# A gated-DeltaNet and RWKV-7 layer on one core: half of the triangular solver's transfers issued by ScalarE instead of SyncE

## The chip, the cores and the metric

The kernel runs on one core of one Trainium2 chip. The metric is the device time of one execution in microseconds (us). TensorE (PE) multiplies matrices, VectorE (DVE), ScalarE (ACT) and GpSimd (POOL) do the elementwise work, and SyncE (SP) has no arithmetic: here it issues transfers. Each engine takes its own instructions strictly in the order in which the program lists them, and waits for another engine, or for a transfer, on semaphores. An instruction that waits holds all that stand behind it on its engine. A transfer is carried out by the core's 16 DMA engines; the engine that issues it is free again once it has issued it.

## The reference

One layer over 512 latent tokens and 256 context tokens of width 2048. A modulated RMSNorm is followed by one input projection. Its columns feed eight gated-DeltaNet heads of width 128 and sixteen RWKV-7 heads of width 64. Both mixers run over the tokens in both directions, context first. Then come a gated output projection, the residual sum and a last RMSNorm. What matters here is the triangular system inside each chunk of 64 tokens:

```python
lmat = jnp.where(strict, jnp.einsum('bhncd,bhnsd->bhncs', kb, k) * decay, 0.0)
eye = jnp.eye(CHUNK, dtype=jnp.float32)
tmat = lax.linalg.triangular_solve(eye + lmat, jnp.broadcast_to(eye, lmat.shape),
                                   left_side=True, lower=True, unit_diagonal=True)
u = tmat @ (v * beta[..., None])
wk = tmat @ (kb * jnp.exp(g)[..., None])
...
def step(state, inp):
    u_i, wk_i, attn_i, q_i, k_i, gl_i = inp
    v_new = u_i - wk_i @ state
    o_i = q_i @ state + attn_i @ v_new
    state = state * jnp.exp(gl_i)[..., None, None] + jnp.einsum('bhcd,bhce->bhde', k_i, v_new)
    return state, o_i
```

The kernel brings RWKV-7 into the same chunked form, so that both mixers need the inverse of unit lower triangular 64x64 blocks, for both directions.

## The kernel before, in words

The heads are worked on in eight slots: a slot has one DeltaNet head and two RWKV-7 heads. Each slot is run twice, first over the context (phase 0, four chunks) and then over the latents (phase 1, eight chunks). So there are sixteen mixers: context slots 0 to 7 and then latent slots 0 to 7. The stages of a mixer are listed in `mixer`: the preparation of both branches (`prep_g`, `prep_r`, `prep_d 0`, `blocks 0`, `prep_d 1`, `blocks 1`), then `send`, `late_g`, `late_r`, `solve`, `levels`, `chain`, and for latents `outp`.

The solver is made of four of them. `blocks` leaves the triangular blocks of direction d in the tile `Z`. `send` gathers the 32x32 diagonal blocks of `Z` into the DRAM tile `DA` with eight transfers, one for each block row b (0 to 3) and direction d (0, 1). `solve` reads `DA` back into `solNL`, with one small matrix on each partition, inverts all of them on DVE in thirty steps of two instructions (`solT` and `solNL`), and writes the inverses and their transposes to the DRAM tile `DD` in one transfer. `levels` reads `DD` back with twelve transfers: for each b one into the tile `RT` (its name in the rows is `lt`) and two into `Z`. Two groups of small matmuls then make the off-diagonal blocks, and ACT and DVE write these into `Z`. `chain` runs over the chunks in order, with a state that goes from one step to the next (`Xs`, `SV`, `vt`, `vn`, `SG` and `Sbd` are its tiles).

Beside the mixers lies work that doesn't depend on them. In phase 0 it is the projections of both streams, in the beginning of phase 1 the rest of the projections, and after that the passes of the output projection. All of it splits each float32 weight tile into a high part `wh` (ACT) and a low part `wl` (DVE or POOL) and runs three matmuls for each product (`accl` and `accc` are the accumulators in the rows).

The order of the instructions is not the order of the code. Every operation is recorded (`record`) with a duration and with its dependences, and `schedule` places all of them by a model of the engines; `emit` writes them in that order. Where PE would have little to do, `schedule` puts in matmuls on a tile of zeros (`wm<-zero` in the rows). They compute nothing that is used. All transfers are recorded on SP with 475 ns each. Since one helper issues every operation, all rows of the profile have one line, L705, and the names tell them apart.

Of the kernel before, what the change touches and what calls it, by code (L numbers as in the profile page):

```python
# [148 lines left out]
OWN = {"V": 120, "A": 148, "G": 107, "S": 1500}  # L149
# [117 lines left out]

class Op:
    __slots__ = ("eng", "fn", "args", "kw", "npred", "succ", "ready", "dur", "tiles", "need", "prio", "idx", "src",
                 "end", "ps", "bytes", "key", "hold", "rows", "passes", "sync", "pos", "load", "fill", "bun", "cells", "cls", "lock")  # L270

    def clone(self):
        o = Op()
# [7 lines left out]
class Rec:  # L281
# [22 lines left out]
    def new(self, eng, fn, args, kw):  # L304
        o = Op()
        o.eng, o.fn, o.args, o.kw = eng, fn, args, kw
        o.npred, o.succ, o.ready, o.tiles, o.need, o.end, o.bytes = 0, [], 0.0, [], [], None, 0
        o.sync, o.load, o.pos, o.fill = [], 0, -1, self.fill if eng == "T" else 0
        o.idx = len(self.ops)
        o.key = o.idx + self.shift  # L310
        o.bun = self.bun if eng == "T" else None
        if o.bun:
            o.bun.ops.append(o)
        o.src = Rec.hook() if Rec.hook else None
        self.ops.append(o)
        return o
# [35 lines left out]
    def record(self, eng, fn, args, kw):  # L352
        o = self.new(eng, fn, args, kw)
        outs, ins = [], []
# [9 lines left out]
        for views, wr in ((ins, False), (outs, True)):  # L364
            for v in views:
                t = v.t
# [11 lines left out]
                for rec in t.acc:  # L378
                    a, apm, afm, aw = rec
# [12 lines left out]
        o.lock = 0  # L392
        o.sync = [a for a, sync in preds.items() if sync and a.eng != eng]
        for a, sync in preds.items():
            if a.eng == eng:
                lat = OWN.get(eng, -1) if sync else -1
            else:
                lat = LAT.get(a.eng + eng, 0) if sync else 0
            self.edge(a, o, lat)
        g = (outs[0] if outs else args[0]).shape if True else None  # L400
        n = int(np.prod(g[1:])) if len(g) > 1 else 1
# [22 lines left out]
        elif eng == "V":  # L424
            x2 = fn.startswith("tensor_scalar") or fn == "tensor_copy"
            x2 = x2 and all(v.t.pool.space != PSUM for v in outs + ins)
            two = sum(v.t.pool.space != PSUM and int(np.prod(v.shape[1:])) > 1 for v in ins) > 1
            o.lock = 2 if x2 else 1 if two else 0
            if fn == "tensor_tensor_scan":
                n *= 2  # L430
            if fn == "reciprocal":
                n *= 7
            if fn == "tensor_reduce":
                n = int(np.prod(ins[0].shape[1:]))
            o.dur = 65 + n / (1.92 if x2 else 0.96) + (62 if sc else 0)
        elif eng == "A":
            sv = isinstance(kw.get("scale"), View) and isinstance(kw.get("bias"), View)
            sc = "accum_out" in kw or any(isinstance(kw.get(a), View) for a in ("scale", "bias"))
            o.dur = (51 if args[1].t.pool.space == PSUM else 93) + 93 * sc + 0.834 * n
        elif eng == "G":  # L440
            o.lock = 1 if fn == "memset" else 2
            a, b = {"memset": (35, 0.84), "tensor_copy": (120, 3.34), "tensor_scalar": (130, 3.8)}.get(fn, (148, 2.104))
            if fn == "tensor_tensor" and any(v.g.ap[-1][0] == 0 for v in ins):
                b = 1.667
            o.dur = (298 + 165 * n) if ALU.pow in args else a + b * n
        elif eng == "S":
            o.dur = 475
            o.bytes = 4 * int(np.prod(args[0].shape)) * (2 if min(run(v) for v in outs + ins) < 128 else 1)

    def schedule(self):  # L450
        ops = self.ops
        end = {}
# [85 lines left out]
        while True:  # L538
# [109 lines left out]
            if e == "P":  # L648
                p = o.args[0]
                if o.fn == "open":  # L650
                    for k, t in p.tags.items():
# [1 line left out]
                        for x in t[1]:  # L653
                            x.free = s
                        wake(p, k)
            if e == "S":
                st = max(fin + 650, dfree)
                dfree = st + o.bytes / 360.0
                fin = dfree + 900
# [9 lines left out]
            extra += o is not ops[o.idx]  # L669
            for t in o.tiles:  # L670
                t.left -= 1
                t.last = max(t.last, fin + (200 if e != "S" else 0))
                if t.left == 0:
                    t.slot.free = t.last
                    wake(t.pool, t.key)
# [35 lines left out]
def run(v):  # L711
    n = 1
    for s, m in list(v.g.ap)[::-1][:len(v.g.ap) - (v.t.pool.space != DRAM)]:
        if m > 1 and s != n:
            break
        n *= m
    return n
# [6 lines left out]
class Mix:  # L724
# [251 lines left out]
    def send(self):  # L976
        k, i, ph, nj, S = self.k, self.i, self.ph, self.nj, self.k.S
        DA, DD = self.DD = [k.dp.tile([w, 4, 2, 3 * nj, 32, 32], F32, tag=f"{t}{ph}", bufs=2, name=k.nm(t))
                            for t, w in (("DA", 1), ("DD", 2))]
        DA = DA[0]  # L980
        for b in range(4):
            for d in range(2):
                S.dma_start(DA[b, d].rearrange("u s t -> s u t"), self.zdiag(b, d))

    def solve(self):
        k, i, ph, nb = self.k, self.i, self.ph, self.nb
# [18 lines left out]
    def levels(self):  # L1005
# [3 lines left out]
        RT = self.t2("lt")[:, 0:96 * nj].rearrange("p (u t) -> p u t", t=32)  # L1009
        for b in range(4):  # L1010
            bb = b % 2
            S.dma_start(RT[32 * b:32 * b + 32], (DN, DL)[bb][b, bb].rearrange("u s t -> s u t"))
            for d in range(2):
                S.dma_start(self.zdiag(b, d), (DL, DN)[d][b, d].rearrange("u s t -> s u t"))
        FC = (slice(32, 64), slice(0, 32))
        px = k.pmt("lx", "g")[:, 0:96 * nj].rearrange("p (u t) -> p u t", t=32)
        with k.rec.bundle():
# [927 lines left out]
```

## Time and profile before

| what | us |
|---|---|
| three runs, median (lowest to highest) | 2066.45 (2064.42 to 2070.24) |
| the profiled execution, its own time | 2065.16 |
| its span | 2063.4 |
| PE busy in it | 1932.1 |
| DVE busy | 1451.6 |
| ACT busy | 811.6 |
| POOL busy | 575.9 |

The span is what the profile covers of the execution; 1.8 us lie around it. Busy times of one engine add up to at most the span. The filler matmuls on zeros count as PE busy. DMA-issuing instructions are not counted as busy on the engine that issues them; rows that begin with SPq have them with their start and the time that they took to issue. The time to landing of a transfer is counted from its issue.

### The profile page before, as it was taken

To read this page: it belongs to the slowest core of one execution; us is meant where nothing else is said; L and a number is where in the kernel's file an instruction comes from. 1 tells how busy PE (TensorE), PEld (TensorE's weight loads), DVE (VectorE), ACT (ScalarE), POOL (GpSimd) and SP (SyncE) were. 2 spreads that over 40 slices of the span, in tenths; PEclk is the share of its full clock that TensorE was granted. 3 is DMA by queue.
4 is the path that set the end of the run, shared out by engine and by line. 5 is a ranking of instruction groups with operands and counts; after the bars stand their busy time and mean duration, and the time that the engine had idled before them with its cause. 6 is when DMAs were issued, how large, how long until landed. Compare 5 with 4: busy or idle time off the path is not lost.

```text
span 2063.4 us, 43525 instructions
## 1 busy us (share of the span) xinstructions
PE 1932.1 (94%) x16575; PEld 1501.0 (73%) x16576; DVE 1451.6 (70%) x3397; ACT 811.6 (39%) x2127; POOL 575.9 (28%) x751
## 2 busy tenths in 40 slices
PE   7999999999999999999999999979778898889997
PEld 5678887877878787777777777767656666666666
DVE  5437587787877678684775784676678877778557
ACT  4443324333232433333443343444435362534335
POOL 0004314223150512100211211245234443343235
PEclk8999999999999999999999999999899999999998
DMA  8964343434333432344543454456232545143732
GB/s 313 362 215 132 107 118 97 111 85 109 91 102 94 106 111 66 99 112 133 159 137 86 120 144 112 125 171 205 74 82 56 164 143 153 52 110 105 257 107 93
DMA packets 230514, 269.28 MB, mean 131 GB/s; under 512 B 117280, under 2 KB 130080, under 8 KB 226208
## 3 DMA queue, kind: packets, MB, share of 16 engines
q1 hardware_dynamic: 230304, 266.49, 43.9%
q8 instruction: 130, 2.13, 0.4%
q14 instruction: 80, 0.66, 0.1%
HBM read 210.50 MB, written 55.89 MB: 129 GB/s over the span
## 4 chain that ended last, share of the span: by engine, by line
PE 68%; DVE 17%; DMA 6%; issue 3%; ACT 3%; POOL 2%; SPq 1%; DVEq 0%; ACTq 0%; POOLq 0%
PE accl L705 37%; PE accc L705 9%; PE br L705 8%; PE wm L705 7%; PE pss L705 7%; DVE solNL L705 3%; DVE Gk L705 2%; DVE solT L705 2%; DVE t L705 1%; SPq L705 1%; POOL gw L705 1%; DVE Z L705 1%; DMA solNL<-DA 1%; DMA gw<-wada 1%; DVE wl L705 1%
## 5 line engine op out<-in xcount | busy, mean ns | idle before, releaser
L705 ACT ACTIVATE wh<-wr 128x512 fp32r<-128x512 f32 x312 | 196.3, 629 | 398.5 <-PE accl L705 180.6
L705 PE MATMUL accl<-hhi,wl 128*128 128x512 f32 x768 | 314.2, 409 | 4.7 <-DVE wl L705 4.7
L705 PE MATMUL accl<-hhi,wh 128*128 128x512 f32 x768 | 310.9, 405 | 1.8 <-issue 1.8
L705 PE MATMUL accl<-hlo,wh 128*128 128x512 f32 x768 | 307.9, 401 | 0.0
L705 DVE TENSOR_TENSOR wl<-wr,wh 128x512 fp32r<-128x512 f32 x264 | 189.6, 720 | 105.7 <-ACT wh L705 99.5
L705 PE MATMUL accl<-yh,wh 128*128 128x512 f32 x480 | 207.8, 435 | 11.0 <-DVE Rr L705 5.4
L705 PE MATMUL accl<-yh,wl 128*128 128x512 f32 x480 | 199.6, 416 | 0.0
L705 PE MATMUL accl<-yl,wh 128*128 128x512 f32 x480 | 197.2, 411 | 0.4 <-POOL yl L705 0.4
L705 DVE TENSOR_TENSOR solNL<-solNL,solT 48x30 f32<-48x30 f32 (+29 forms) x480 | 171.4, 357 | 10.6
L705 PEld LDWEIGHTS accl<-hhi,wl 128*128 128x128 f32 x768 | 144.5, 188 | 41.7 <-DVE wl L705 6.6
L705 POOL TENSOR_TENSOR SRd<-Sbd,Dd 64x128 f32<-64x128 f32 x160 | 67.2, 420 | 379.1 <-DVE Sbd L705 372.9
L705 DVE TENSOR_TENSOR solT<-solNL 48x30 f32<-48x30 f32 (+29 forms) x480 | 165.8, 346 | 10.0
L705 PEld LDWEIGHTS accl<-hhi,wh 128*128 128x128 f32 x768 | 144.4, 188 | 20.9 <-issue 4.8
L705 PEld LDWEIGHTS accl<-hlo,wh 128*128 128x128 f32 x768 | 144.6, 188 | 19.7 <-issue 3.3
L705 PE MATMUL accc<-clo,wh 128*128 128x256 f32 x512 | 147.8, 289 | 0.0
L705 PE MATMUL accc<-chi,wh 128*128 128x256 f32 x512 | 146.2, 286 | 0.0
L705 PE MATMUL accc<-chi,wl 128*128 128x256 f32 x512 | 146.1, 285 | 0.0
L705 PE MATMUL wm<-zero 128*128 128x128 bf16 x1326 | 105.8, 232 | 22.8 <-DVE SG L705 7.7
L705 PEld LDWEIGHTS <-zero 128*128 128x128 bf16 x1344 | 91.2, 105 | 40.7 <-issue 36.1
L705 PEld LDWEIGHTS accl<-yh,wh 128*128 128x128 f32 x480 | 91.2, 191 | 36.6 <-issue 11.3
L705 PEld LDWEIGHTS accc<-clo,wh 128*128 128x128 f32 x512 | 96.4, 188 | 23.3 <-issue 0.5
L705 PEld LDWEIGHTS accc<-chi,wh 128*128 128x128 f32 x512 | 96.5, 189 | 20.8 <-issue 0.3
(320 smaller groups left out, 4139.2 us busy)
## 6 DMA issues: line engine op xcount, KB each, us to landing
wr<-win SPq DMA_DIRECT2D x256, 256.0 KB, 3.2
wa<-wada SPq DMA_DIRECT2D x32, 1024.0 KB, 6.3
gw<-wada SPq DMA_DIRECT2D x64, 256.0 KB, 3.5
ud<-Gk SPq DMA_DIRECT2D x64, 256.0 KB, 2.9
wr<-wout SPq DMA_DIRECT2D x64, 256.0 KB, 3.6
Rk<-ud SPq DMA_DIRECT2D x48, 256.0 KB, 3.0
rtd<-xt SPq DMA_DIRECT2D x48, 256.0 KB, 3.1
Rr<-rtd SPq DMA_DIRECT2D x48, 256.0 KB, 3.1
```

The lines of the kernel that those rows point to most:

```text
L705: r = getattr(self.engs[o.eng], o.fn)(*args, **kw)
```

## The change

The four transfers of `send` for direction 1, and the six transfers of `levels` for the block rows 1 and 3, are issued by ACT. All others stay on SP. Each mixer thus has 10 transfers on ACT, and all sixteen have 160. The model of `schedule` learns that an operation of any engine can be a transfer (the new field `dq`): on ACT it takes 300 ns of the engine, on SP 475 ns as before, and its landing is modelled in the same way. Everything else is recorded as before, but since `schedule` places all operations anew, the order of the instructions changes on every engine.

```diff
@@ def new
+        o.dq = fn == "dma_start"
@@ def record
-            if a.eng == eng:
-                lat = OWN.get(eng, -1) if sync else -1
+            src, dst = "S" if a.dq else a.eng, "S" if o.dq else eng
+            if src == dst == "S" or (a.eng == eng and not a.dq):
+                lat = OWN.get(src, -1) if sync else -1
             else:
-                lat = LAT.get(a.eng + eng, 0) if sync else 0
+                lat = LAT.get(src + dst, 0) if sync else 0
...
+        elif o.dq:
+            o.dur = 475 if eng == "S" else 300
+            o.bytes = 4 * int(np.prod(args[0].shape)) * (2 if min(run(v) for v in outs + ins) < 128 else 1)
...
-        elif eng == "S":
-            o.dur = 475
-            o.bytes = 4 * int(np.prod(args[0].shape)) * (2 if min(run(v) for v in outs + ins) < 128 else 1)
@@ def schedule
-            if e == "S":
+            if o.dq:
                 st = max(fin + 650, dfree)
                 dfree = st + o.bytes / 360.0
                 fin = dfree + 900
...
-                t.last = max(t.last, fin + (200 if e != "S" else 0))
+                t.last = max(t.last, fin + (0 if o.dq else 200))
@@ def send
         for b in range(4):
             for d in range(2):
-                S.dma_start(DA[b, d].rearrange("u s t -> s u t"), self.zdiag(b, d))
+                (S, k.A)[d].dma_start(DA[b, d].rearrange("u s t -> s u t"), self.zdiag(b, d))
@@ def levels
         for b in range(4):
             bb = b % 2
-            S.dma_start(RT[32 * b:32 * b + 32], (DN, DL)[bb][b, bb].rearrange("u s t -> s u t"))
+            q = (S, k.A)[b % 2]
+            q.dma_start(RT[32 * b:32 * b + 32], (DN, DL)[bb][b, bb].rearrange("u s t -> s u t"))
             for d in range(2):
-                S.dma_start(self.zdiag(b, d), (DL, DN)[d][b, d].rearrange("u s t -> s u t"))
+                q.dma_start(self.zdiag(b, d), (DL, DN)[d][b, d].rearrange("u s t -> s u t"))
```

What stands on the engines can be shown at latent slot 4. On SP, this is the read-back of `levels` before (`lt` and `Z` out of `DD`; `lr`, `Rk` and `rtd` belong to other work):

```order
L705 DMA lr_0_9325<-lorad_114 96x512
L705 DMA lt_0_9336<-DD_0_124 32x12x32
L705 DMA Z_0_9361<-DD_0_124 32x12x32 x2
L705 DMA lt_0_9336<-DD_0_124 32x12x32
L705 DMA Z_0_9361<-DD_0_124 32x12x32 x2
L705 DMA lt_0_9336<-DD_0_124 32x12x32
L705 DMA Z_0_9361<-DD_0_124 32x12x32 x2
L705 DMA lt_0_9336<-DD_0_124 32x12x32
L705 DMA Z_0_9361<-DD_0_124 32x12x32 x2
L705 DMA Rk_0_9311<-ud_115 128x512
```

and the same place on SP now:

```order
L707 DMA lr_0_9310<-lorad_114 96x512
L707 DMA lt_0_9321<-DD_0_124 32x12x32
L707 DMA Z_0_9346<-DD_0_124 32x12x32 x2
L707 DMA lt_0_9321<-DD_0_124 32x12x32
L707 DMA Z_0_9346<-DD_0_124 32x12x32 x2
L707 DMA Rr_1_12537<-rtd_117 128x512
```

Twelve transfers have become six, and the transfer behind them follows at once. The other six now stand on ACT, between the split of a weight tile (`wh`) and a tanh of the preparation of slot 5 (`t`):

```order
L707 ACTIVATE wh_1_1437<-wr_1_1434 128x512
L707 DMA lt_0_9321<-DD_0_124 32x12x32
L707 DMA Z_0_9346<-DD_0_124 32x12x32 x2
L707 DMA lt_0_9321<-DD_0_124 32x12x32
L707 DMA Z_0_9346<-DD_0_124 32x12x32 x2
L707 ACTIVATE t_2_9306<-br_1_135,dv_66 128x512
L707 ACTIVATE xt_1_12539<-accl_0_144 128x512
```

The second place is where `chain` of slot 4 begins, on ACT. `Z<-pss` is the last step of `levels`, `Xs`, `vt`, `SV` and `vn` are the chain's first step, and `VO`, `junk` and `t` prepare slot 5. Before:

```order
L705 ACTIVATE xt_1_12492<-accl_0_144 128x512
L705 ACTIVATE Z_0_9361<-pss_0_130 32x12x32 x2
L705 ACTIVATE VO_0_12497<-br_1_135 64x4x128 x2
L705 ACTIVATE junk_0_9317,rk_0_9326<-br_0_134 128x128 x4
L705 ACTIVATE t_3_9322<-Rk_0_9311,par_62 128x512
L705 ACTIVATE Xs_0_9342<-pss_0_130 128x256
L705 ACTIVATE vt_0_9345<-wm_0_129,BT_0_71 128x128
L705 ACTIVATE vn_0_9346<-wm_0_129,BS_0_70 128x128
L705 ACTIVATE SV_0_9369<-pss_0_130 64x128
```

and now:

```order
L707 ACTIVATE xt_1_12539<-accl_0_144 128x512
L707 ACTIVATE Z_0_9346<-pss_0_130 32x12x32 x2
L707 DMA DA_1_123<-Z_0_12549 32x12x32 x2
L707 ACTIVATE Xs_0_9327<-pss_0_130 128x256
L707 ACTIVATE vt_0_9330<-wm_0_129,BT_0_71 128x128
L707 ACTIVATE SV_0_9354<-pss_0_130 64x128
L707 ACTIVATE vn_0_9331<-wm_0_129,BS_0_70 128x128
L707 DMA DA_1_123<-Z_0_12549 32x12x32 x2
L707 ACTIVATE VO_0_12544<-br_0_134 64x4x128 x2
```

The gathering of direction 1 for slot 5 (`DA<-Z`) now stands in two pairs before and behind the first step of the chain of slot 4, and `VO`, `junk` and `t` have moved behind that step. Over the whole program PE has 1285 filler matmuls `wm<-zero` where it had 1326; every other kind of instruction has the same count, but for the 160 transfers.

## Rows read from the trace of the kernel before

**Rows 1.** The page's first part: busy time of each engine, its share of the span, and the number of its instructions.

```profile
PE 1932.1 (94%) x16575; PEld 1501.0 (73%) x16576; DVE 1451.6 (70%) x3397; ACT 811.6 (39%) x2127; POOL 575.9 (28%) x751
```

**Rows 2.** Busy time by stretch: the context mixers, the latent slots 0 and 1, and the rest (from us to us, length, busy us and number of instructions of PE, PEld, DVE, ACT and POOL, granted clock, DMA share, GB/s).

```profile
150.00:885.00 735.00, 721.32 (x5525) 591.85 (x5523) 542.23 (x1335) 256.77 (x683) 212.68 (x257) 1.00 0.37 102
885.00:1300.00 415.00, 411.71 (x2991) 315.18 (x2991) 277.33 (x622) 169.03 (x424) 65.54 (x103) 1.00 0.45 125
1300.00:2063.00 763.00, 662.16 (x6836) 496.58 (x6834) 562.33 (x1294) 325.84 (x919) 295.00 (x381) 0.95 0.44 127
```

**Rows 3.** The same stretches, for the instructions on the tile of zeros alone (PE, PEld and POOL, then as above).

```profile
150.00:885.00 735.00, 2.04 (x34) 1.86 (x32) 0.00 (x0) 1.00 0.37 102
885.00:1300.00 415.00, 1.16 (x3) 0.31 (x4) 0.00 (x0) 1.00 0.45 125
1300.00:2063.00 763.00, 89.15 (x1062) 71.38 (x1062) 0.00 (x0) 0.95 0.44 127
```

**Rows 4.** The timeline of SP's queue around the read-back of latent slot 0 (start, time to issue, transfer, count).

```profile
1082.50 0.33 SPq L705 DMA_DIRECT2D lt<-DD  x1
1082.88 0.97 SPq L705 DMA_DIRECT2D Z<-DD  x2
...
1087.48 0.98 SPq L705 DMA_DIRECT2D Z<-DD  x2
```

**Rows 5.** The chain of work that ended last, in order of time (start, us, what), at the read-backs of the latent slots 2, 4 and 6.

```profile
1442.55 6.01 DMA DD<-solNL
1448.62 0.32 SPq L705
...
1456.47 0.59 SPq L705
1457.15 3.44 DMA dg<-growd
...
1638.82 5.31 DMA lr<-lorad
...
1645.11 2.06 DMA lt<-DD
1647.21 0.97 PE wm L705 x63
...
1852.01 2.09 DMA lt<-DD
1854.14 1.13 PE wm L705 x64
```

**Rows 6.** The same chain at the read-backs of the latent slots 3, 5 and 7.

```profile
1532.04 4.18 DMA Gz<-ud
...
1743.99 2.19 POOL yl L705
1746.17 1.86 POOL KR L705 x4
...
1927.75 5.31 PE accl L705 x21
```

**Rows 7.** Busy time while SP issues the read-backs of the latent slots 0, 2, 4 and 6 (columns as in rows 2).

```profile
1082.50:1088.50 6.00, 6.00 (x27) 4.81 (x27) 1.98 (x3) 2.13 (x4) 0.00 (x0) 1.00 0.66 119
1448.60:1456.90 8.30, 5.37 (x43) 4.38 (x44) 2.07 (x3) 3.32 (x6) 1.11 (x2) 0.75 0.66 137
1639.30:1646.60 7.30, 7.01 (x45) 5.10 (x43) 6.46 (x9) 1.99 (x4) 4.34 (x4) 1.00 0.95 188
1845.70:1853.50 7.80, 7.80 (x31) 5.46 (x29) 5.39 (x8) 2.81 (x6) 4.73 (x4) 1.00 0.78 165
```

**Rows 8.** The read-back into `Z` for the latents, in the view of the transfers (count, KB each, median us from issue to landing).

```profile
Z<-DD SPq DMA_DIRECT2D x64, 48.0 KB, 2.1
```

**Rows 9.** What the gathering costs its queue: the issue time of its instructions (ns, least, median, most), and the waits of SP's queue that VectorE's writes of `Z` ended last (us in total, times, longest).

```profile
L705 SPq DMA_DIRECT2D DA<-Z x128: 302/432/2000, 253.0 to 1862.9; - x128
...
SPq L705 <- DVE Z L705: 75.8, 36, 10.5
```

**Rows 10.** The timeline of ACT in latent slot 2, at `VO` and `junk` and then from the end of `levels` to the chain's first step.

```profile
1445.55 1.20 ACT L705 ACTIVATE VO<-br 64x512 f32<-64x512 f32 x2 [6.85 <-PE br L705]
1446.77 0.28 ACT L705 ACTIVATE junk<-br 128x128 bf16<-128x128 f32 x1
1446.94 0.19 ACT L705 ACTIVATION_READ_ACCUMULATOR junk<-br 128x1 f32 x1
...
1448.24 0.71 ACT L705 ACTIVATE t<-Rk,par 128x512 f32<-128x512 f32 x1
...
1462.27 0.98 ACT L705 ACTIVATE Z<-pss 32x384 f32<-32x384 f32 x2 [1.89 <-PE pss L705]
...
1467.14 0.37 ACT L705 ACTIVATE Xs<-pss 128x256 f32<-128x256 f32 x1
```

**Rows 11.** The timeline of SP's queue at latent slot 4: the inverses are sent to `DD`, and the read-back begins (columns as in rows 4).

```profile
1632.15 0.41 SPq L705 DMA_DIRECT2D DD<-solNL  x1
...
1639.32 0.42 SPq L705 DMA_DIRECT2D lt<-DD  x1
```

More of the change, by code (lines that the diff above doesn't have):

```diff
@@ L269 @@
     __slots__ = ("eng", "fn", "args", "kw", "npred", "succ", "ready", "dur", "tiles", "need", "prio", "idx", "src",
-                 "end", "ps", "bytes", "key", "hold", "rows", "passes", "sync", "pos", "load", "fill", "bun", "cells", "cls", "lock")
+                 "end", "ps", "bytes", "key", "hold", "rows", "passes", "sync", "pos", "load", "fill", "bun", "cells", "cls", "lock", "dq")
     def clone(self):
```

## The prediction

> **What bounds the kernel now.** I read the page's first part first: TensorE is busy for 1932.1 us of 2063.4, VectorE for 70%, ScalarE for 39% [rows 1]. So ScalarE has room on average, and PE is the engine to beat. Averages hide the stages, so the next view is busy time by stretch. From 150 to 885 us (context mixers) PE is busy for 721.3 us of 735, and from 885 to 1300 us (latent slots 0 and 1) for 411.7 of 415 [rows 2], with 2.0 and 1.2 us of fillers in these [rows 3]. There the projections fill every wait of the solver. From 1300 us to the end PE is busy for 662.2 us of 763, and 89.2 of these are fillers. So 763 - 662.2 + 89.2 = 190 us of this stretch hold no useful work of PE. The latent slots 2 to 7 run there, and only there can a shorter solver shorten the kernel.
>
> The third view is the chain of waits in that stretch. At the read-backs of slots 2, 4 and 6 it runs through SP's issues of `levels`: in slot 2 from the landing of `DD` through the issues and on to 1457 us, in slots 4 and 6 through SP to the landing of an `lt`, for which the matmul on `lt` starts (1647.21 and 1854.14 us) [rows 5]. At slots 3, 5 and 7 it goes by other things: the load of a `Gz`, POOL's `yl` and `KR`, the output projection on PE [rows 6].
>
> **The read-back.** Undisturbed, its twelve issues last from 1082.50 to 1087.48 + 0.98 = 1088.46, 5.96 us [rows 4], about 0.5 us each, while one such transfer lands 2.1 us after its issue [rows 8]. So the issue is the larger part. In slots 2, 4 and 6 other transfers mix in and the twelve take some 8.3, 7.3 and 7.8 us [rows 7]. With six on each of two queues the issue could be halved: at most 3.0 us saved. But the DMA engines are busy for 0.66 of the undisturbed six microseconds [rows 7], so the same packets need at least 0.66 x 6 = 4.0 us: 2.0 saved by that bound. In slots 4 and 6 the share is 0.95 and 0.78, with other loads in it, and those could wait. At the other end nothing is saved, if two queues don't issue side by side. I take 2.5 us for each of slots 2, 4 and 6, between 2.0 and the 3.0 to 4.2 that half of the disturbed issues would be: -7.5 us (bounds 0 and -12). For slots 3, 5 and 7 I take nothing, since another wait ends last there; if all three counted it would be another -7.5. For the ten mixers before 1300 us I take nothing: PE is the cover, with 14 us of idle in 735 and 3 in 415. If that cover were thinner, half of the 14 + 3 us would be the most that there is.
>
> The Trainium skill speaks against the change here ("DMA: Bandwidth & Descriptors", "Issuing engines are not separate DMA queues"): transfers of all engines interleave on the same 16 DMA engines, and a second issuing engine saves only the issue time, "which is usually small relative to the DMA itself". Its first half agrees with the DMA share of 0.66 [rows 7]. The second half doesn't hold here, since 12 issues take 5.96 us and one landing 2.1. By that rule taken whole, the term would be near 0 instead of -7.5.
>
> **The gathering.** `send` is split by direction, not by block row. Direction 0 is ready well before direction 1 in the order of the stages, and the solve waits for the last pair of direction 1. That pair goes through one queue before and after, with 2 x 0.43 us of issue [rows 9]. So the split shortens nothing on the path by itself. What it does is free SP from waiting for VectorE's `Z`: 75.8 us in 36 waits, 2.1 us each, up to 10.5 [rows 9]. On SP such a wait holds loads; on ScalarE it will hold arithmetic. I take 0 for the relief of SP (bounds 0 and -7: the stalls of the chain on `lr` before the read-back of slot 4, 5.3 us [rows 5], and half of the `Gz` at slot 3, 4.2 us [rows 6]).
>
> **ScalarE's time.** 160 transfers are added. No row shows one issued by ScalarE. The nearest price is SP's, 0.43 us [rows 9], so 69 us over the kernel or 4.3 per mixer. From below it is the planner's own 0.3 us, from above SP's longest, 2.0. I take SP's median. ScalarE is busy for 326 us of the last 763 [rows 2], so most of it lies in idle time. Where it doesn't: for slots 2 to 6 the order puts two gatherings of the next slot between the end of `levels` and `Xs`, the chain's first step. Two cost 0.86 us, five times 4.3. Against that, in slot 4 `VO`, four `junk` and `t` have left that place. In slot 2 these took 1.20, four times 0.28 + 0.19, and 0.71 us [rows 10], 3.8 in all; they were run while PE had other work, so I count no gain for that. The other pair stands behind the first step's last operation on ScalarE, and the six read-backs stand where the weights' splits run ahead. Waiting comes on top where `Z` is late: 2.1 us as on SP, in 36 of 128 gatherings, which for five pairs is 5 x 2.1 x 0.28 = 3. Of 4.3 + 3 I take 3 us as seen by the end, since `Xs` also waits for PE (bounds 0 and +20, worked out below).
>
> **Fillers.** 41 filler matmuls fewer are in the order. In the last stretch one takes 89.15 / 1062 = 0.084 us [rows 3], so 3.4 us. They fill the waits that the first term shortens, so this is not added. It has the sign and the size of the sum.
>
> **Sum.** -7.5 + 0 + 3 = -4.5 us. The profiled execution took 2065.16 us (span 2063.4 and 1.8 around it), so 2060.7; it lies 1.3 us below the median of the three runs. From the median, 2066.45 - 4.5 = 2062 us.
>
> **Rivals.** (1) *SP was the wider bottleneck.* Freed of the waits and the 160 issues, it brings the loads of slots 2 to 7 earlier as well. All six read-backs count (-15) with the relief of -7 and the cost of +3, -19 at most; with some of it given back on ScalarE I put it at -15, 2051 us. For it: in slot 4 `DD` was issued at 1632.15 us and the read-back at 1639.32 [rows 11], behind other loads. Against it: the chain goes elsewhere at slots 3, 5 and 7 [rows 6], where VectorE's 562 us in 763 [rows 2] limits what can be moved up.
>
> (2) *ScalarE is held in the chain; slower.* The place is the pair of `DA` between the end of `levels` and `Xs`, and the pair behind `vn`. If ScalarE reaches them before VectorE has written `Z`, the state's step waits, PE with it, and the splits that feed the output projection too. The price: each pair 0.86 + 2.1 us, two pairs, five slots: 29.6 us at the most. With two thirds of it seen, +20, and the read-back's -7.5, it is +12: 2078 us. It decides from a mean wait of some 0.7 us a pair on (ten pairs: 7.5 us, the gain). For it: on SP 36 of 128 gatherings were waited for. Against it: the order was made for ScalarE this time, and in slot 2 `Xs` started 4.9 us after `Z` on ScalarE anyhow [rows 10].
>
> (3) *The second queue issues nothing faster*, because the two queues take turns at making the packets' lists: twelve issues still take 6 us, each on ScalarE twice as long while SP issues too. The gain is gone, and 3 us of cost remain: 2066.45 + 0 to 3, say 2068 us. For it: SP issues back to back at 0.5 us each though the DMA engines are not full (0.66). Against it: nothing in these rows shows two queues. The Trainium skill has this as a rule ("Perfetto Trace Analysis", "DMA Instruction — HWDGE (DVE, Sync)"): the block that generates descriptors is shared by two sequencers and locked for exclusive use. The trace can't show it, as all transfers were issued by SP.
>
> **How the numbers follow.** The forecast has 0.42, rival 1 0.22, rival 2 0.22, rival 3 0.14. A measurement of this kernel tells a change of 0.3%, 6.2 us, from none. The forecast alone spans 2052 to 2068 and lies just inside that bound, so of its 0.42 I give 0.18 to faster, 0.22 to same, 0.02 to slower. Rival 1 is faster (0.22). Rival 2 is slower with 0.20, same with 0.02. Rival 3 is same with 0.12, slower with 0.02. So faster 0.40, same 0.36, slower 0.24. The range runs from below rival 1 to rival 2, 2046 to 2079 us.
>
> **What would show it.** The issues of `levels` on SP should last about 3 us instead of 6, with ScalarE's six beside them, and the DMA share in them should go from 0.66 to near 1. ScalarE's transfers should take about 0.43 us each. PE's fillers after 1300 us should be about 3 us fewer, and the idle of PE between 885 and 1300 us unchanged. If ScalarE's issues take 0.9 us beside SP's 0.9, rival 3 is right; if `Xs` starts later behind `Z` than the 4.9 us from start to start in slot 2, with ScalarE waiting for `DA<-Z`, rival 2. The prediction is wrong if the time leaves 2052 to 2068, and its reason is wrong if the read-back doesn't get shorter, whatever the time.

## The result and the profile after

The changed kernel takes 2098.49 us (median of four runs, 2092.79 to 2100.36), the kernel before 2068.34 in the four runs that go with it: a ratio of 1.0143, interval 1.0114 to 1.0171. It is slower by 1.4%, where 2062 us were predicted, and above the range. The profiled execution took 2092.79 us, with a span of 2090.9.

The page of the kernel after, first and third part: busy time of each engine, and the transfer queues (packets, MB, share of 16 engines).

```profile
PE 1937.9 (93%) x16535; PEld 1500.6 (72%) x16535; DVE 1449.8 (69%) x3397; ACT 809.8 (39%) x2127; POOL 583.9 (28%) x751
...
q1 hardware_dynamic: 181664, 260.59, 41.2%
q10 hardware_dynamic: 48640, 5.91, 1.9%
```

The engines do what they did in [rows 1], to within 1.4% (POOL) and 0.3% (all others). The second queue (q10) carries a fifth of the packets but 2% of the bytes: the 160 transfers are small. PE is busy 5.8 us longer with 40 instructions fewer; the other 21.7 of the 27.5 us that the span is longer are waiting. The same stretches as in [rows 2]:

```profile
150.00:885.00 735.00, 718.91 (x5511) 588.53 (x5510) 541.04 (x1333) 255.73 (x679) 212.07 (x257) 1.00 0.37 101
885.00:1300.00 415.00, 411.97 (x3018) 314.98 (x3016) 275.60 (x625) 170.34 (x429) 68.47 (x106) 1.00 0.44 124
1300.00:2063.00 763.00, 654.42 (x6629) 485.04 (x6629) 543.88 (x1260) 312.81 (x889) 285.24 (x365) 0.94 0.42 123
```

Up to 1300 us little has changed: PE's idle time between 885 and 1300 us is 3.0 us where it was 3.3. After it every engine has done less by 2063 us, DVE 18 us less. The clock is 0.94 instead of 0.95.

One number per slot shows where the time goes: the start of the first matmul on `lt`, which ends the wait for the read-back. In latent slots 0 to 7 it moved by -7.2, -4.5, +1.4, +8.2, +19.7, +21.7, +26.3 and +31.1 us. From slot 0 to slot 7 the kernel after is 38.4 us slower, 2.1 to 11.5 a slot; all but the first 2.7 us of it (slot 0 to 1) lies where the prediction looked for a gain. Each such round has three parts, read from the timelines at `solNL<-DA` (the solve reads its blocks), `DD<-solNL` (the inverses leave) and the matmul on `lt`. Their sums over slots 1 to 7, in us (one profiled execution of each kernel):

| | `lt` to next read of `DA` | read to `DD` | `DD` to `lt` | sum |
|---|---|---|---|---|
| before | 274.5 | 468.0 | 98.9 | 841.4 |
| after | 287.7 | 481.4 | 110.7 | 879.8 |

**The issue did get shorter.** The read-back of latent slot 0 on the two queues, SP's first and ScalarE's behind it (start, time to issue; for ScalarE's arithmetic in brackets its idle time and what ended it):

```profile
1078.46 0.34 SPq L707 DMA_DIRECT2D lt<-DD  x1
1078.85 1.41 SPq L707 DMA_DIRECT2D Z<-DD  x2
1080.37 0.39 SPq L707 DMA_DIRECT2D lt<-DD  x1
1081.82 0.95 SPq L707 DMA_DIRECT2D Z<-DD  x2
```

```profile
1078.42 0.36 ACTq L707 DMA_DIRECT2D lt<-DD  x1
1078.81 1.46 ACTq L707 DMA_DIRECT2D Z<-DD  x2
1080.31 0.53 ACTq L707 DMA_DIRECT2D lt<-DD  x1
1081.44 1.00 ACTq L707 DMA_DIRECT2D Z<-DD  x2
1082.57 1.16 ACT L707 ACTIVATE wh<-wr 128x512 fp32r<-128x512 f32 x2 [5.00 <-DMA lt<-DD]
```

Twelve issues take 4.35 us (1078.42 to 1082.77) instead of 5.96 [rows 4], side by side. The first eight take 2.41 us (to 1080.83), where one queue took 3.92; the last four are held up, by what is told below. The DMA engines are not full in that time, at a share of 0.79 (columns as in [rows 2]):

```profile
1078.42:1082.77 4.35, 4.35 (x20) 3.53 (x19) 0.00 (x0) 0.20 (x1) 0.00 (x0) 1.00 0.79 151
```

In slots 2, 4 and 6, where the gain was looked for, the twelve take 5.3, 8.1 and 6.3 us; before they took 7.2, 7.3 and 7.8. The last row of ScalarE's timeline holds the price: `wh`, an operation that has nothing to do with the solver, waited 5.00 us on ScalarE, because ScalarE stood at its first `lt` until `DD` had landed, and then issued.

**Held ScalarE delays the read-back that it serves.** Latent slot 2, ScalarE's timeline:

```profile
1444.13 0.93 ACTq L707 DMA_DIRECT2D DA<-Z  x1
1448.95 0.31 ACTq L707 DMA_DIRECT2D lt<-DD  x1
...
1453.14 1.19 ACT L707 ACTIVATE VO<-br 64x512 f32<-64x512 f32 x2 [8.49 <-DMA lt<-DD]
...
1454.62 0.59 ACT L707 ACTIVATE xt<-accl 128x512 f32<-128x512 f32 x1
```

`DD` was sent on SP, and SP's first `lt` went out 1.7 us ahead of ScalarE's:

```profile
1438.39 1.34 SPq L707 DMA_DIRECT2D DD<-solNL  x1
...
1447.29 0.33 SPq L707 DMA_DIRECT2D lt<-DD  x1
```

PE's timeline of the same slot, and PE's waits for `xt` in slots 4 and 6:

```profile
1455.27 2.08 PE L707 MATMUL accl<-Rr,cst 128*128 128x512 f32 x2 [8.49 <-ACT xt L707]
...
1459.19 1.27 PE L707 MATMUL wm<-lt,Z 32*32 32x32 f32 x96
...
1660.23 1.13 PE L707 MATMUL accl<-Rr,cst 128*128 128x512 f32 x2 [4.12 <-ACT xt L707]
...
1873.68 2.08 PE L707 MATMUL accl<-Rr,cst 128*128 128x512 f32 x2 [2.68 <-ACT xt L707]
```

In the kernel before, `DD` of slot 2 was sent at 1442.55 us [rows 5], and the matmul on `lt` came here:

```profile
1457.78 1.50 PE L705 MATMUL wm<-lt,Z 32*32 32x32 f32 x96
```

What PE waited for longest after 1300 us (us in total, times, longest), and the same wait in the kernel before:

```profile
PE accl L707 <- ACT xt L707: 16.3, 5, 8.5
...
PE accl L705 <- ACT xt L705: 1.2, 3, 0.5
```

The chain of waits there (start, us, what):

```profile
1444.13 7.01 DMA DA<-Z
1451.15 0.02 issue
1451.16 1.99 DMA lt<-DD
1453.15 0.11 ACT VO L707
...
1454.72 0.50 ACT xt L707
1455.22 0.04 issue
1455.27 2.08 PE accl L707 x2
1457.34 3.15 PE wm L707 x104
```

ScalarE sits at its transfers from 1445 to 1453 us. `xt`, which empties an accumulator of PE, stands behind them, PE's `accl` waits for `xt`, and in PE's order `accl` stands ahead of the matmuls on `lt`. So the read-back has long been issued when PE takes it up: its last transfer landed at 1454.89 us, 4.3 us earlier. The same in slots 4 and 6, where ScalarE's first arithmetic behind the transfers (`t`) had waited 6.07 and 4.70 us, and PE 4.12 and 2.68 us for `xt`. From `DD` to the matmul on `lt` slots 2, 4 and 6 take 20.8, 18.9 and 18.6 us; before they took 15.2, 13.8 and 13.4.

The chain shows a second tie. SP's `lt` at 1451.16 us started when ScalarE's `DA<-Z`, issued at 1444.13 and of another slot, had landed. In the program all transfers of both queues use the same eight completion semaphores in turn (155 or 156 transfers on each, by the trace), and each waits until the one that used its semaphore last has landed. So never more than eight transfers are under way, in either kernel, and the two queues are not independent.

One queue hardly feels that: in the kernel before, 4 of the 96 read-back transfers of the latent slots went out within 0.11 us of such a landing, so on its signal. In the kernel after it is 43 of 96, the last four of slot 0 among them (1081.44 to 1082.47 us). In slot 0 this tie, more than the issue, keeps two queues from halving the read-back. It is also most of what holds ScalarE there. Taken transfer by transfer (the timeline merges some pairs and hides the gaps in them), ScalarE stands idle in front of its read-backs for 21.3 us after 1300 us. For 5.1 of these `DD` had not landed; for the other 16.2 it had, and ScalarE waited for a semaphore. In slot 2 `DD` landed at 1447.27 us, but ScalarE's first `lt` went out at 1448.95, when the `DA<-Z` that it had issued at 1441.07 had landed (1448.87). The tie alone does not make a kernel slow, though: the fastest version below (e3) has 41 of 96 such transfers.

ScalarE's waits for transfers after 1300 us:

```profile
ACT yh L707 <- DMA yl<-yd: 46.1, 10, 11.3
...
ACT t L707 <- DMA lt<-DD: 8.5, 2, 4.7
ACT VO L707 <- DMA lt<-DD: 8.5, 1, 8.5
...
ACT t L707 <- DMA Z<-DD: 6.1, 1, 6.1
ACT wh L707 <- DMA Z<-DD: 5.5, 1, 5.5
```

The lower four are new, 28.6 us; each is the whole time from one operation to the next, with the issues in it, and stands under the name of the transfer that the page saw last. `yh` waited less before:

```profile
ACT yh L705 <- DMA yl<-yd: 26.0, 5, 7.9
```

From the timeline as it merges them, ScalarE's idle time in front of its own transfers after 1300 us adds up to 31.7 us: 13.7 before the gathering (where it waits for `Z`), 12.2 before `lt`, 5.8 before `Z`. The experiments below use this count.

### The profile page after: what moved, and what is told of

Its sections match the earlier page's. It is cut to its first block, busy times and chain, and to the rows that moved or that the text cites. A ratio compares the mean times of both kernels' runs of the same rounds, so it can differ in the third digit from the quotient of the medians.

```text
span 2090.9 us, 43352 instructions
## 1 busy us (share of the span) xinstructions
PE 1937.9 (93%) x16535; PEld 1500.6 (72%) x16535; DVE 1449.8 (69%) x3397; ACT 809.8 (39%) x2127; POOL 583.9 (28%) x751
## 4 chain that ended last, share of the span: by engine, by line
PE 68%; DVE 13%; DMA 7%; ACT 4%; issue 3%; POOL 2%; SPq 1%; ACTq 0%; DVEq 0%; POOLq 0%
PE accl L707 37%; PE accc L707 9%; PE br L707 8%; PE wm L707 7%; PE pss L707 6%; DVE solNL L707 2%; DVE Gk L707 1%; DVE Z L707 1%; DVE t L707 1%; SPq L707 1%; DVE solT L707 1%; DVE ot L707 1%; DMA Z<-DD 1%; DMA yl<-yd 1%; DVE Sbd L707 1%
## 5 line engine op out<-in xcount | busy, mean ns | idle before, releaser
L707 PE MATMUL accl<-yh,wh 128*128 128x512 f32 x480 | 209.7, 439 | 11.2 <-DVE Rr L707 7.6
L707 DVE TENSOR_TENSOR solNL<-solNL,solT 48x30 f32<-48x30 f32 (+29 forms) x480 | 165.3, 344 | 10.6
L707 PEld LDWEIGHTS accl<-yh,wh 128*128 128x128 f32 x480 | 92.2, 193 | 39.6 <-issue 13.1
```

What stands on the lines that cost most here:

```text
L707: r = getattr(self.engs[o.eng], o.fn)(*args, **kw)
```

## The experiments

Ratios are against the kernel before in the same sitting (runs taken together), with a 95% interval. Each run has a short name, given in brackets, by which it is called later on.

**Queue and order apart.** The change does two things: ScalarE issues, and everything is planned anew. So each order was run with either queue. On the order after, with all on SP (e1):

```diff
-            r = getattr(self.engs[o.eng], o.fn)(*args, **kw)
+            r = getattr(self.engs["S" if o.dq else o.eng], o.fn)(*args, **kw)
```

> The order of the changed kernel on every engine, but SP issues all 160 transfers at the places that the order gives them. Theory hold (ScalarE is held by its transfers, in the read-backs and in the gatherings): the loss goes, 2060 to 2078 us. Rival order (the new order of all engines is worse by itself, whoever issues): 2090 to 2105 us.

2096.2 us, 1.014 (1.0083 to 1.0197). On the order before, with the same 160 transfers (marked `alt`) issued by ScalarE (e2):

```diff
-            r = getattr(self.engs[o.eng], o.fn)(*args, **kw)
+            r = getattr(self.engs["A" if o.alt else o.eng], o.fn)(*args, **kw)
```

> The order of the kernel before on every engine, but ScalarE issues the same 160 transfers, at the places where they stand in that order. Theory hold: as slow as the changed kernel or slower, 2090 to 2130 us, since the order was not made for ScalarE. Rival order: near the kernel before, 2060 to 2075 us.

2067.0 us, 1.001 (0.9984 to 1.0037). Both come out as the rival order has it: the time goes with the order, not with the engine that issues. In e1, `DD` to `lt` is short, 85.6 us in all, and PE's `accl` hardly waits for `xt`:

```profile
PE accl L707 <- ACT xt L707: 1.0, 2, 0.5
```

But from `lt` to the next read of `DA` it takes 311.4 us instead of 287.7. The gathering is not what comes late there: over the seven rounds its last transfer follows the last write of `Z` by 11.2 us in all, 11.3 in the kernel after. It is that write, the end of the next slot's preparation, that comes 27.9 us later behind `lt`, and why is not shown. SP now has the waits of all 160 transfers, so e1 doesn't show what the order costs without any hold.

**One part alone**, planned anew. Only the read-back on ScalarE (e3):

```diff
-                (S, k.A)[d].dma_start(DA[b, d].rearrange("u s t -> s u t"), self.zdiag(b, d))
+                S.dma_start(DA[b, d].rearrange("u s t -> s u t"), self.zdiag(b, d))
```

> Only the read-back of block rows 1 and 3 is on ScalarE, the gathering is all on SP; the order is planned anew for it. If the hold in the read-back makes the loss: 2085 to 2105 us. If the gathering beside the chain makes it: 2060 to 2072 us.

2055.1 us, 0.9945 (0.9916 to 0.9975): the fastest version here, and below both expectations. Only the gathering on ScalarE (e4):

```diff
-            q = (S, k.A)[b % 2]
+            q = S
```

> Only the gathering of direction 1 is on ScalarE, the read-back is all on SP; the order is planned anew for it. If the hold in the read-back makes the loss: 2062 to 2075 us. If the gathering beside the chain makes it: 2080 to 2100 us.

2078.3 us, 1.0043 (1.0012 to 1.0073), between the two expectations. Both parts together lose 1.4%, so the parts don't add up.

**Is it the luck of one order?** The kernel before, planned with another price for a transfer on SP, 465 ns (n1):

```diff
-            o.dur = 475
+            o.dur = 465
```

> The kernel before, all transfers on SP, but the planner counts 465 ns for a transfer in place of 475: no work and no queue changes, only the order. Theory luck (a new order moves the time by a per cent by itself, either way): anywhere from 2045 to 2090 us. Rival cause (the orders made for ScalarE's transfers are worse for a reason): within 8 us of the kernel before.

2070.4 us, 1.0014 (0.9983 to 1.0045); with 490 (n2):

> As the run with 465 ns, with 490 ns. Luck: anywhere from 2045 to 2090 us, and not the same as with 465. Rival cause: within 8 us of the kernel before.

2064.1 us, 1.0003 (0.9979 to 1.0027). Both lie within 8 us of the kernel before, as the rival cause has it. And the kernel after, with ScalarE's price at 430, what the trace shows, instead of 300 (a1):

```diff
-            o.dur = 475 if eng == "S" else 300
+            o.dur = 475 if eng == "S" else 430
```

> The changed kernel, planned with the 430 ns that ScalarE's transfers were seen to take, in place of 300. Luck: anywhere from 2050 to 2100 us. Rival cause, of the kind that the planner's price was too low: 2062 to 2075 us. Rival cause, of the kind that the gathering sits badly on ScalarE whatever its price: 2085 to 2105 us.

2088.2 us, 1.0115 (1.007 to 1.016); with 250 (a2):

> The changed kernel, planned with 250 ns for ScalarE's transfers. Luck: anywhere from 2050 to 2100 us. Rival cause of either kind: 2090 to 2110 us.

2095.0 us, 1.0134 (1.0085 to 1.0184). Three prices, three orders, all slow: it is not one unlucky order, and the wrong price explains little of it.

**Transfers planned as ready later**, so that ScalarE is given other work ahead of them. First the gathering (h1):

```diff
             else:
                 lat = LAT.get(src + dst, 0) if sync else 0
+            if o.dq and eng == "A" and sync and args[1].t.pool.space != DRAM:
+                lat += 2500
```

> The changed kernel, with one thing else: while the order is planned, a gathering on ScalarE counts as ready 2.5 us after its `Z` is written, so other work of ScalarE is put ahead of it. In the changed kernel ScalarE stands idle in front of its transfers for 31.7 us after 1300 us: 13.7 before the gathering, 12.2 before `lt`, 5.8 before `Z` of the read-back. Theory A (ScalarE is held at the heads of the gathering): the 13.7 us fall to 5 or less and the time falls to 2075 to 2085 us. Theory B (it is held at the read-back, where it waits for `DD` to land): the 18.0 us before `lt` and `Z` stay and the time stays within 2090 to 2102. Theory C (the waits in front of the transfers are harmless, and the order of the other work costs): the idle time falls and the time stays within 2090 to 2102 us.

2087.3 us, 1.0118 (1.0051 to 1.0185), between the ranges of the three theories. The idle time in front of the gathering fell from 13.7 to 0.7 us, that before `lt` and `Z` from 18.0 to 7.7. The seven latent rounds now take 842.0 us, as before the change, but the loss has moved into the context, where the clock and PE's busy time fell:

```profile
150.00:885.00 735.00, 712.64 (x5311) 587.57 (x5310) 527.50 (x1280) 246.61 (x647) 213.65 (x249) 0.98 0.36 100
```

The first matmul on `lt` of latent slot 0 starts at 1112.5 us, against 1084.8 in the kernel after. The condition with `==`, for the read-back (h2):

> The changed kernel, with a read-back on ScalarE counted as ready 2.5 us later while the order is planned, the gathering as in the changed kernel. Theory A (held at the gathering): 2090 to 2102 us. Theory B (held at the read-back): the 18.0 us of idle time before `lt` and `Z` on ScalarE fall to 8 or less, as in the kernel with the read-back alone (7.0), and the time falls to 2075 to 2085. Theory C (order of the rest): the idle time falls, the time doesn't.

2080.5 us, 1.0071 (1.0046 to 1.0097), with 9.0 us of idle time before `lt` and `Z` (in the shortest of its ten runs, 2068.6 us, which is the one profiled): theory B, in part. Without the last condition, for both (h3):

> The changed kernel, with both kinds of transfers on ScalarE counted as ready 2.5 us later while the order is planned. Theories A and B together (ScalarE held in front of its transfers): the 31.7 us of idle time fall below 15 and the time falls to 2055 to 2075 us. Theory C (the order of the rest costs, whoever is held): the time stays above 2085 although the idle time falls.

2064.2 us, 0.9993 (0.9964 to 1.0023). The idle time fell to 11.4 us and the loss is gone. That fits theories A and B, but this edit, too, plans everything anew. `DD` to `lt` is no shorter in it (112.5 us); the gain lies in the other two parts. Its rows come from the longest of its ten runs (2073.6 us).

**The same with the order held.** In d1 the order after is kept on every engine, and only ScalarE's transfers are put further back, after the planning:

```diff
+            if o.dq and o.eng == "A":
+                held.append((min(s + 2500, o.end), s, o))
+            else:
+                late.append((s, o))
```

> The order of the changed kernel exactly as planned, in which only ScalarE's own transfers are moved: each stands up to 2.5 us of planned time later, behind ScalarE's operations of that stretch, but ahead of whatever needs it. All arithmetic, on every engine, and SP's transfers stay in the order of the changed kernel (2098 us). Theory A+B (arithmetic of ScalarE is held behind transfers that wait for their source): the idle time in front of ScalarE's transfers after 1300 us falls from 31.7 us to 15 or less and the time falls by 10 us or more, to 2088 or less. Theory C (the order of the arithmetic and of SP's transfers costs, not the holding): the time stays within 2090 to 2102 us.

2089.6 us, 1.0129 (1.0099 to 1.0159). It falls between the theories, and the interval overlaps with that of the kernel after. So the time by itself doesn't show that the holding costs. The profile tells more: the idle time fell to 13.1 us, and PE's wait for `xt` and the read-back recovered (the helper's line is L719 in this kernel).

```profile
PE accl L719 <- ACT xt L719: 5.3, 4, 3.7
```

`DD` to `lt` is 90.5 us instead of 110.7, with 14.9, 14.1 and 12.5 in slots 2, 4 and 6. So the delay of the read-back in the kernel after was ScalarE being held. But from `lt` to the next read it is 299.3 us instead of 287.7, and the seven rounds take 863.2, still 21.8 above before. Not all of that rest is the order of the other work: the edit puts the gathering later as well, and its last transfer follows the last write of `Z` by 22.2 us over the seven rounds instead of 11.3. If all of the 11.6 us between 287.7 and 299.3 come from that, 10.2 are left for the order; this is an estimate, and no run separates the two.

**The read-back by itself, in the order before** (q1):

```diff
+            k.rec.alt = bb == 1
             S.dma_start(RT[32 * b:32 * b + 32], (DN, DL)[bb][b, bb].rearrange("u s t -> s u t"))
```

> The order of the kernel before exactly as planned, in which ScalarE issues half of the read-backs (96 transfers) and SP all else. If the shorter issue of the read-back is worth what the prediction took, 2.5 us in each of slots 2, 4 and 6: 2057 to 2061 us, ratio about 0.9965. If the second queue gains nothing unless the order is planned for it: within 0.2% of before.

2068.4 us, 1.0016 (0.9998 to 1.0034). No gain: the twelve issues take 5.9, 6.7 and 7.2 us in slots 2, 4 and 6, 2.4 less in all than before, but `DD` to `lt` is 14.8, 13.8 and 13.3 us, 0.5 less in all. ScalarE's timeline in slot 0 shows what its transfers stand behind:

```profile
1088.77 0.63 ACT L707 ACTIVATE wh<-wr 128x512 fp32r<-128x512 f32 x1 [2.17 <-PE accl L707]
1089.02 0.34 ACTq L707 DMA_DIRECT2D lt<-DD  x1
...
1091.57 0.63 ACT L707 ACTIVATE wh<-wr 128x512 fp32r<-128x512 f32 x1 [1.68 <-DMA Z<-DD]
1091.68 0.31 ACTq L707 DMA_DIRECT2D lt<-DD  x1
...
1094.37 0.63 ACT L707 ACTIVATE wh<-wr 128x512 fp32r<-128x512 f32 x1 [2.17 <-PE accl L707]
1094.38 0.31 ACTq L707 DMA_DIRECT2D Z<-DD  x1
```

Its six transfers stand among splits `wh` that start 2.80 us apart, in step with PE (the page puts the middle wait down to a transfer), so they last from 1089.02 to 1094.69 us, nearly as long as the twelve did on SP. And the other way round, the order of e3 with all transfers on SP (r1, the edit of e1):

> The order of the kernel with the read-back alone on ScalarE (2055 us, ratio 0.9945), but every transfer is issued by SP. If the second queue gains the 0.5%, by the shorter issue of the read-backs: back at 2064 to 2072 us, with twelve issues of 6 to 8 us in each read-back. If the order gains it, whoever issues: 2052 to 2060.

2057.9 us, 0.9973 (0.9953 to 0.9994), against 0.9945 (0.9916 to 0.9975) with two queues. `DD` to `lt` is 92.1 us with one queue and 90.8 with two. The order carries about half of e3's gain, and by the intervals it may be all of it.

**How far do orders spread?** The kernel of e3, planned with its transfers on ScalarE 2.5 us later (b1, the lines of h3):

> The kernel with the read-back alone on ScalarE (2055 us, ratio 0.9945), planned with its read-backs on ScalarE counted as ready 2.5 us later. There ScalarE stands idle in front of them for 7.0 us only after 1300 us. Theory A+B: 2047 to 2056 us, a little faster or the same, since little is left to be taken away. If the later place of the read-backs on ScalarE costs more than the holding: above 2060 us.

2087.7 us, 1.0121 (1.0102 to 1.0139). A clear miss for theories A and B: little idle time to take away (7.0 us, now 9.5), and some 32 us lost. The kernel before, all on SP, with the gathering of direction 1 (marked `alt`) planned 2.5 us later (c1):

```diff
+            if o.alt and sync:
+                lat += 2500
```

> The kernel before, all transfers on SP, with the gathering of direction 1 counted as ready 2.5 us later while the order is planned: a disturbance of the planner as large as those that moved the kernels with ScalarE's transfers, and no second queue. Theory D (any disturbance of this size spreads the planned orders by a per cent or so, whoever issues): the time leaves 2058 to 2072 us in either direction. Theory E (orders become slow only where transfers are planned on ScalarE): the time stays within 2058 to 2072.

2067.7 us, 1.0004 (0.9975 to 1.0032): as theory E has it. At last, both kernels planned with later landings of all transfers (g1 the kernel after, g2 the kernel before):

```diff
-                fin = dfree + 900
+                fin = dfree + 2400
```

> The changed kernel, planned with every transfer, on either queue, landing 1.5 us later, which is nearer to the landings that the trace shows for `DD` (2.6 us in the middle, up to 8.9). If the order of the changed kernel is slow because the planner takes transfers to land too early and ScalarE is held by what they bring (86 us of waits for transfers on ScalarE from the read-back of latent slot 0 on, against 54 before): these waits fall below 60 us and the time falls to 2060 to 2080. If it is the spread of orders: anything from 2055 to 2100, without a tie to these waits.

> The kernel before, planned with every transfer landing 1.5 us later. If the planner's early landings cost in the order of before as well: faster than before, 2045 to 2060 us. If the order of before suits the landings as they are: 2060 to 2070. Above 2075 it is theory D, the spread of orders, without any transfer on ScalarE.

The kernel after: 2111.0 us, 1.022 (1.0173 to 1.0266), although ScalarE's waits for transfers, counted as in the expectation, fell from 86 to 38 us. So these waits as a whole don't set its time, and the expectation that tied it to them missed. The kernel before: 2100.3 us, 1.0152 (1.0099 to 1.0204), with no transfer on ScalarE. Its latent rounds take 845.0 us; its loss lies in the context, as in h1 (first matmul on `lt` of latent slot 0 at 1116.9 us, 1092.0 before). Small disturbances left the order before within 0.2%, this one cost 1.5%: theory E falls. An order from this planner can be 1.5% slower for reasons that have nothing to do with a second queue.

## Why the prediction was wrong, point by point

- **What bounds the kernel**: right. Before 1300 us PE stayed covered, and all but 2.7 of the 38.4 us lost from slot 0 to slot 7 lie in latent slots 2 to 7.
- **The read-back, -7.5 us**: this is the step that failed first. That two queues issue side by side was right (4.35 us against 5.96 in slot 0, a saving of 1.6 where 2.5 were taken). In slots 2, 4 and 6 together the issues got 2.6 us shorter, not 7.5: the sum took the issue and the DMA engines as the only bounds, and not the eight transfers that can be under way. (The 8.3 us of slot 2 held two other issues; the twelve took 7.2.) That this shortens slots 2, 4 and 6 was wrong: they took 5.6, 5.1 and 5.2 us more from `DD` to `lt`, 16 us in all, as ScalarE was held with PE's `xt` behind it; slots 1, 3, 5 and 7 took 4.2 us less together, where the sum had nothing. With the order kept, q1 saves 0.5 us in slots 2, 4 and 6 instead of 7.5. The chain went through SP's issues [rows 5], but what came next on PE and ScalarE was hardly earlier.
- **The rule of the Trainium skill** weighed there ("DMA: Bandwidth & Descriptors", "Issuing engines are not separate DMA queues") gave a term near 0. In the order kept that is what came out, though for another reason than its page gives: the twelve issues together were longer than one landing (5.96 against 2.1 us), and were not the last thing waited for. The DMA share of 0.66, which was read as agreeing with its first half, came from one queue and could not bear on it.
- **The gathering, 0 for SP's relief**: not refuted. In e2 the part from `lt` to the next read is 5.6 us shorter, and the time is the same.
- **ScalarE's time, +3 us**: the price per transfer was right, the waits were mis-sized:

```profile
L707 ACTq DMA_DIRECT2D DA<-Z x64: 309/452/2522, 265.3 to 1892.3; - x64
L707 ACTq DMA_DIRECT2D Z<-DD x64: 309/426/937, 310.0 to 1962.9; - x64
```

  The medians are 0.45 and 0.43 us (0.43 were taken). But 3 us of waiting were counted, for the gathering alone (by its own numbers 6, as a pair has two gatherings); it was 31.7 us, 18.0 of it at the read-back, for which none was counted. That ScalarE would wait at the read-back, for `DD` to land and, for longer, for a semaphore to come free, was not thought of: on SP such a wait holds loads, on ScalarE it holds `xt`, and PE waits for that.
- **Fillers**: to the end of the kernel they take 86.35 us after 1300 us instead of 89.15 [rows 3], 2.8 less (3.4 were taken), and they are a sign of nothing: the kernel is slower.
- **Rivals.** Rival 3 is out: in slot 0 the first `lt` of both queues go out within 0.04 us of each other, in 0.34 and 0.36 us, and 60 of ScalarE's 96 read-back transfers, issued while SP was issuing for over half of the time, took 0.45 us in the median, where one queue took 0.46 before. The exclusive lock that the Trainium skill describes ("Perfetto Trace Analysis", "DMA Instruction — HWDGE (DVE, Sync)") doesn't show between SP and ScalarE here. Rival 1 didn't come. Rival 2 had the direction and the cause of a part, with the place wrong: not the pair of `DA` ahead of `Xs` (from the matmul on `lt` to the first `Xs` the kernel after takes 7.2 to 11.0 us, before 7.2 to 11.7, though ScalarE stood 2.52 us in front of that pair in slots 4, 5 and 6), but the read-back itself.
- **What no rival had**: that planning everything anew can by itself cost 1 to 2%. The sum moved a few instructions and left the rest in place. e1 and e2 show that the loss comes with the new order, whoever issues; g2 and b1 show that a new order can cost as much by itself. How much of the loss is the order of the other work is known only within bounds: in d1 21.8 of 38.4 us of the latent rounds stay when ScalarE's transfers are moved out of the way, and up to 11.6 of these can be d1's own. Which of the many moved operations carry it stays open; from `lt` to the next read and from there to `DD` the kernel after loses 13.2 and 13.4 us, and no single wait has most of that (in the first, 8.1 us go by as the next slot's `Z` is written later behind `lt`, and 3.2 as it is gathered later behind that).

## What to carry to other kernels

A transfer that is moved to an engine with arithmetic costs not its issue but its wait: look at what must land before it (its source, and the transfer that used its semaphore last), what stands behind it on that engine, and who waits for that. Count the transfers that can be under way before a second queue is taken to halve the time: here eight. Where a planner makes the order anew, run the new order with the old queue and the old order with the new queue before the queue is given the credit or the blame; here the loss came with the new order on either queue, and about half of the best version's gain came with its order alone. A shorter issue pays only if the next thing on the path is ready for it.

## What was not expected of the hardware

Two queues issue side by side, each at about the price of one alone (0.45 against 0.46 us in the read-backs). Transfers of different queues are still tied by the completion semaphores that they share: SP's `lt` waited for the landing of ScalarE's `DA<-Z`, 7.01 us after its issue. And the spread between runs of one kernel goes with the mean granted clock: of 19 runs of the kernel before in one sitting, the shortest took 2055.32 us at a clock of 0.984, the longest 2082.25 at 0.968.

The clock adds to a late transfer. Three stretches of the kernel after in slot 2 (columns as in [rows 2]):

```profile
1445.00:1450.00 5.00, 1.77 (x7) 0.84 (x5) 0.00 (x0) 0.00 (x0) 1.04 (x2) 0.96 0.82 220
1450.00:1455.00 5.00, 0.00 (x0) 0.00 (x0) 0.00 (x0) 1.83 (x5) 0.00 (x0) 0.50 0.78 148
1455.00:1460.00 5.00, 4.74 (x87) 3.32 (x90) 0.69 (x1) 2.22 (x9) 2.45 (x3) 0.51 0.81 273
```

PE waits for `xt` and does nothing from 1450 to 1455 us; when it runs again, its clock is at the lower of its two levels (0.51, 1.2 GHz). The two matmuls that had waited take 2.08 us here and 1.02 us at 1445.69. So what waits behind a late transfer then also runs at half speed.
